# Attention scores in a single-core encoder block: both heads of a tile together, and K's low part against 64 rows of Q

## The chip, the core and the metric

The kernel runs on one core of one Trainium2 chip. The metric is the device time of one execution in microseconds. The arithmetic of the projections is done in fp32r matmuls on a high and a low part of each number, so that two or three passes give nearly float32 products.

## The reference

One layer of a hybrid encoder, 256 tokens, width 2048. The attention branch, which the change touches, has 16 heads of 64 on 4 key/value heads, a window of 128 tokens either way and a sink per head; around it stand large projections.

```python
u = rmsnorm(h, norm_mix_g)
z = u @ w_in                                   # 2048 -> 8704
b_a, c_a, v_a, q, k, v, gl_a, gl_b = split(z)
y_a = (b_a * centred_dwconv3(c_a * v_a, conv_a_w)) @ w_out_a
q, k = rope(q), rope(k)
scores = (q @ k.T) * HEAD_DIM ** -0.5          # masked to |kpos - qpos| <= 128
m = max(max(scores), sink)
p = exp(scores - m) / (sum(exp(scores - m)) + exp(sink - m))
y_b = (p @ v) @ w_o_attn
h = h + (sigmoid(gl_a + ba) * y_a + sigmoid(gl_b + bb) * y_b) @ w_mix_out
up = centred_dwconv3(rmsnorm(h) @ ffn_w_up, ffn_conv_w) + ffn_conv_b
h = h + (silu(a) * gv) @ ffn_w_down            # a, gv = halves of up
return rmsnorm(h, norm_final_g)
```

## The kernel before

**The projections.** Weights are streamed from HBM in chunks of eight 128x128 blocks. ScalarE rounds a chunk to fp32r (`whi`, L166), VectorE takes the rest (`wlo`, L177), and TensorE makes for each block one matmul of 512 columns with `whi` (L197: high and low part of the activations side by side) and one of 256 columns with `wlo` (L198). The last block of a job has its `whi` matmul in L202. `run` (from L105 on) walks over the chunks. After each chunk it raises `now` by one and calls `run_due`, which first advances the generators under way (each `yield` hands on to the next chunk) and then begins what is due at this chunk, in the order in which it was entered. Instructions go to each engine's queue in the order written.

**The attention.** A tile `t` (0 to 7) is a pair of heads `e` = 0, 1 that share their place in a 128-row block of Q. `rope` leaves for each head a tile in which rows `64*e` to `64*e+63` are the head's 64 dimensions and the other 64 rows are a copy of them. `rope_q` (L384 on) makes the first 64 rows the high part of Q and the other 64 the low part (L386, L390), so that one matmul over 128 rows of `qs` against `kh`, whose halves are both K's high part, gives (Q high + Q low) x K high. `kl`, K's low part, stands in both halves too. `att_scores(t, e)` multiplies, for each of two blocks `n` of 128 queries, `qs` with `kh` (L422) and then with `kl` (L423) into one bank of PSUM, `s0` or `s1` by head, with one buffer each. Then come the mask, the maximum, the exponential and the division (L428 to L444). `att_turn` transposes the probabilities (L452), `att_out` multiplies them with V (L465): there the two heads of a tile go to different halves of the output's partitions, so that each matmul uses 64 columns of the array.

**The order.** A table at the end of the attention's code enters the five steps of tile `t` at chunk 29 + 21t/4 (whole chunks, so 5 or 6 apart) plus 0 for `att_scores(t, 0)`, 3 for `att_scores(t, 1)`, 5 and 8 for the two turns, 10 for the output. They lie between the projections of `w_in`.

Of the kernel before, what the change touches and what calls it, by code (L numbers as in the profile page):

```python
# [7 lines left out]
F32 = mybir.dt.float32  # L8
# [6 lines left out]
P = 128  # L15
D = 2048
T = 256
# [34 lines left out]
def hybrid_block_kernel(ctx: ExitStack, tc: tile.TileContext, head, wide, xT, w_in, w_oa, w_o, w_mix, w_up, w_dn, vec, cst, out):  # L52
    nc = tc.nc
# [5 lines left out]
    aps = ctx.enter_context(tc.tile_pool(name="aps", bufs=1, space=PSUM))  # L59
# [9 lines left out]
    def col(i):  # L69
        return vt[:, i : i + 1]  # L70
# [17 lines left out]
    def at(n, fn):  # L88
        due.append((n, count[0], fn))
        count[0] += 1  # L90
# [257 lines left out]
    qs = p1.tile([P, 4, 2, 2, T], F32R, tag="qs", name="qs")  # L348
    kh = p1.tile([P, 2, 2, T], F32R, tag="kh", name="kh")
    kl = p1.tile([P, 2, 2, T], F32R, tag="kl", name="kl")  # L350
# [63 lines left out]
    probs = {}  # L414
    mask = ct[:, C_MASK : C_MASK + T]

    def att_scores(t, e):
        kv = t // 4
        sc = aps.tile([P, 2, T], F32, tag=f"s{e}", name=f"s{e}")
        for n in range(2):  # L420
            q = qs[:, t // 2, e, t % 2, n * P : (n + 1) * P]
            nc.tensor.matmul(sc[:, n, :], q, kh[:, e, kv, :], start=True, stop=False)  # L422
            nc.tensor.matmul(sc[:, n, :], q, kl[:, e, kv, :], start=False, stop=True)  # L423
        h = PAIRS[t][e]
        sink, ns = col(V_SINK + h), nsink[:, h : h + 1]
        flat = sc.rearrange("p n t -> p (n t)")

        nc.vector.tensor_tensor(flat[:, P : 3 * P], flat[:, P : 3 * P], mask, op=ALU.add)  # L428
        st = p1.tile([P, 8], F32, tag="st", name="st", bufs=4)
        mx, nm, den, es = (st[:, 2 * i : 2 * i + 2] for i in range(4))  # L430
        nc.vector.tensor_reduce(mx, sc, axis=AX.X, op=ALU.max, negate=True)
        nc.vector.tensor_scalar(nm, mx, HD**-0.5, ns, op0=ALU.mult, op1=ALU.min)
        yield 1
        p = p1.tile([P, 2, T], F32, tag="p", name="p", bufs=3)
        for n in range(2):
            nc.scalar.activation(
                p[:, n, :], sc[:, n, :], AF.Exp, bias=nm[:, n : n + 1], scale=HD**-0.5, accum_out=den[:, n : n + 1]
            )
        nc.scalar.activation(es, nm, AF.Exp, bias=sink)
        yield 1  # L440
        nc.vector.tensor_tensor(den, den, es, op=ALU.add)
        nc.vector.reciprocal(den, den)
        for n in range(2):
            nc.vector.tensor_scalar(p[:, n, :], p[:, n, :], den[:, n : n + 1], None, op0=ALU.mult)  # L444
        probs[t, e] = p

    def att_turn(t, e):
        p = probs.pop((t, e))
        tp = aps.tile([P, 2, T], F32, tag="tp", name="ptp")
        for b in range(2):  # L450
            for n in range(2):
                nc.tensor.transpose(tp[:, b, n * P : (n + 1) * P], p[:, n, b * P : (b + 1) * P], ident)  # L452
        yield 1
        pT = p1.tile([P, 2, T], F32, tag="pT", name="pT", bufs=2)
        nc.scalar.copy(pT, tp)
        probs[t, e] = pT

    def att_out(t):
        kv = t // 4
        o = aps.tile([P, 2 * T], F32, tag="av", name="av")  # L460
        pT = [probs.pop((t, e)) for e in range(2)]
        for b in range(2):
            for e in range(2):
                v0 = 128 * kv + 64 * e
                nc.tensor.matmul(  # L465
                    o[64 * e : 64 * e + 64, 0:T], vtok[:, b, v0 : v0 + HD], pT[e][:, b, :], start=b == 0, stop=b == 1
                )
        yield 1
        yield from split(box["B"][:, 8 + t, :], o[:, 0:T])
# [65 lines left out]
        at(40 + 4 * i, lambda i=i: nc.sync.dma_start(x[:, 4 * i : 4 * i + 4, :], xT[:, 4 * i : 4 * i + 4, :]))  # L535
    for t in range(8):
        for n, fn in (
            (0, lambda t=t: att_scores(t, 0)),
            (3, lambda t=t: att_scores(t, 1)),
            (5, lambda t=t: att_turn(t, 0)),  # L540
            (8, lambda t=t: att_turn(t, 1)),
            (10, lambda t=t: att_out(t)),
        ):
            at(29 + 21 * t // 4 + n, fn)
# [290 lines left out]
```

## Time and profile before

| | |
|---|---|
| median of 3 runs | 1354.29 us (1352.67 to 1354.65) |
| the profiled execution, its time | 1353.56 us |
| its span in the trace | 1351.8 us |
| mean granted TensorE clock | 0.998 of full |
| PE busy | 1340.5 us, 7687 instructions |
| PEld busy (weight loads, beside PE) | 1163.5 us |
| DVE busy | 971.5 us |
| ACT busy | 711.2 us |

The span is what the core's instructions take; 1.8 us lie around it. The scores are computed between 77 and 207 us of the span. A matmul's row in the trace begins when TensorE takes it up and its end is modelled, so that rows overlap: the time that a matmul costs is read from its start to the start of the next one, or from the chain, which cuts the rows where they overlap.

### The profile page before, as it was taken

To read this page: it belongs to the slowest core of one execution; us is meant where nothing else is said; L and a number is where in the kernel's file an instruction comes from. 1 tells how busy PE (TensorE), PEld (TensorE's weight loads), DVE (VectorE), ACT (ScalarE), POOL (GpSimd) and SP (SyncE) were. 2 spreads that over 40 slices of the span, in tenths; PEclk is the share of its full clock that TensorE was granted. 3 is DMA by queue.
4 is the path that set the end of the run, shared out by engine and by line. 5 is a ranking of instruction groups with operands and counts; after the bars stand their busy time and mean duration, and the time that the engine had idled before them with its cause. 6 is when DMAs were issued, how large, how long until landed. Compare 5 with 4: busy or idle time off the path is not lost.

```text
span 1351.8 us, 20512 instructions
## 1 busy us (share of the span) xinstructions
PE 1340.5 (99%) x7687; PEld 1163.5 (86%) x7687; DVE 971.5 (72%) x1544; ACT 711.2 (53%) x1120; POOL 58.6 (4%) x66
## 2 busy tenths in 40 slices
PE   9999999999999999999999999999999999999997
PEld 8888888888888888888888888888888888888886
DVE  7999887555557887668888888888888865555554
ACT  7656665544445554456555555555555544444441
POOL 0000000000000003420000000000000001001001
PEclk9999999999999999999999999999999999999999
DMA  8776545555555547547555555555555557656663
GB/s 296 231 226 197 188 154 178 184 186 186 187 186 187 187 133 239 186 135 235 186 187 186 187 184 188 186 187 185 186 185 187 169 155 234 187 180 187 187 188 100
DMA packets 75876, 254.23 MB, mean 188 GB/s; under 512 B 8704, under 2 KB 9088, under 8 KB 75776
## 3 DMA queue, kind: packets, MB, share of 16 engines
q1 hardware_dynamic: 75488, 252.52, 58.8%
q8 instruction: 60, 0.98, 0.3%
q10 hardware_dynamic: 288, 0.39, 0.1%
q14 instruction: 40, 0.33, 0.1%
HBM read 248.16 MB, written 2.10 MB: 185 GB/s over the span
## 4 chain that ended last, share of the span: by engine, by line
PE 99%; DVE 0%; DMA 0%; ACT 0%; issue 0%; POOLq 0%; DVEq 0%; ACTq 0%
PE ps L197 60%; PE ps L198 33%; PE ps L202 4%; PE av L465 1%; PE ptp L452 1%; PE ps L200 0%; PE s L423 0%; PE s L422 0%; DMA hd<-in_head_dram 0%; PE more L657 0%; POOLq L830 0%; DVE y L699 0%; DVE r L691 0%; DVE x L664 0%; PE nps L240 0%
## 5 line engine op out<-in xcount | busy, mean ns | idle before, releaser
L177 DVE TENSOR_TENSOR wlo<-raw,whi 128x1024 fp32r<-128x1024 f32 (+2 forms) x494 | 570.8, 1158 | 324.9 <-PE ps L198 230.5
L166 ACT CAST whi<-raw 128x1024 fp32r<-128x1024 f32 (+2 forms) x494 | 488.2, 989 | 349.2 <-PE ps L197 180.0
L197 PE MATMUL ps<-hs,whi 128*128 128x512 f32 x1320 | 470.1, 399 | 0.0
L198 PE MATMUL ps<-hs,wlo 128*128 128x256 f32 x1408 | 381.2, 281 | 0.0
L197 PE MATMUL ps<-xs,whi 128*128 128x512 f32 x1020 | 363.9, 399 | 0.6 <-DVE xs L320 0.6
L197 PEld LDWEIGHTS ps<-hs,whi 128*128 128x128 f32 x1320 | 248.1, 188 | 57.1
L198 PE MATMUL ps<-xs,wlo 128*128 128x256 f32 x1088 | 295.4, 281 | 0.0
L198 PEld LDWEIGHTS ps<-hs,wlo 128*128 128x128 f32 x1408 | 265.8, 189 | 8.9
L197 PEld LDWEIGHTS ps<-xs,whi 128*128 128x128 f32 x1020 | 192.3, 189 | 44.3 <-ACT whi L166 0.9
L198 PEld LDWEIGHTS ps<-xs,wlo 128*128 128x128 f32 x1088 | 206.1, 189 | 5.6 <-DVE wlo L177 0.3
L226 ACT COPY evb<-ps 128x256 f32<-128x256 f32 x188 | 69.7, 372 | 212.2 <-PE ps L202 208.5
L197 PE MATMUL ps<-actC,whi 128*128 128x512 f32 x405 | 143.8, 399 | 0.0
L198 PE MATMUL ps<-actC,wlo 128*128 128x256 f32 x448 | 122.3, 281 | 0.0
L197 PEld LDWEIGHTS ps<-actC,whi 128*128 128x128 f32 x405 | 76.1, 188 | 18.9
L197 PE MATMUL ps<-ms,whi 128*128 128x512 f32 x240 | 85.4, 399 | 0.0
L198 PEld LDWEIGHTS ps<-actC,wlo 128*128 128x128 f32 x448 | 84.7, 189 | 0.8
L197 PE MATMUL ps<-actA,whi 128*128 128x512 f32 x240 | 85.3, 398 | 0.0
L197 PE MATMUL ps<-ya_att,whi 128*128 128x512 f32 x224 | 80.4, 398 | 0.0
L230 DVE TENSOR_TENSOR evt<-ps,evb 128x256 f32<-128x256 f32 x178 | 74.5, 418 | 0.0
L198 PE MATMUL ps<-actA,wlo 128*128 128x256 f32 x256 | 71.1, 281 | 0.0
L198 PE MATMUL ps<-ms,wlo 128*128 128x256 f32 x256 | 69.3, 281 | 0.0
L198 PE MATMUL ps<-ya_att,wlo 128*128 128x256 f32 x256 | 66.6, 281 | 0.0
(149 smaller groups left out, 1159.1 us busy)
## 6 DMA issues: line engine op xcount, KB each, us to landing
raw<-in_w_up_dram SPq DMA_DIRECT2D x170, 512.0 KB, 4.5
raw<-in_w_in_dram SPq DMA_DIRECT2D x124, 512.0 KB, 4.7
raw<-in_w_dn_dram SPq DMA_DIRECT2D x70, 512.0 KB, 4.1
raw<-in_w_mix_dram SPq DMA_DIRECT2D x26, 512.0 KB, 4.8
raw<-in_w_dn_dram SPq DMA_DIRECT2D x36, 256.0 KB, 2.7
raw<-in_w_oa_dram SPq DMA_DIRECT2D x16, 512.0 KB, 3.6
raw<-in_w_o_dram SPq DMA_DIRECT2D x16, 512.0 KB, 3.6
raw<-in_wide_dram SPq DMA_DIRECT2D x15, 512.0 KB, 5.3
```

The lines of the kernel that those rows point to most:

```text
L166: nc.scalar.copy(his[c][:, a:b, :], raws[c](a, b))
L177: nc.vector.tensor_tensor(los[c][:, a:b, :], raw(a, b), his[c][:, a:b, :], op=ALU.subtract)
L197: nc.tensor.matmul(ps, hi[:, i, :], a, start=k == 0, stop=False)
L198: nc.tensor.matmul(ps[:, 0:T], lo[:, i, :], a[:, 0:T], start=False, stop=False)
L202: nc.tensor.matmul(ps, hi[:, i, :], a, start=False, stop=True)
L226: nc.scalar.copy(b, ps[:, T : 2 * T])
L230: nc.vector.tensor_tensor(dst, ps[:, 0:T], b, op=ALU.add)
L452: nc.tensor.transpose(tp[:, b, n * P : (n + 1) * P], p[:, n, b * P : (b + 1) * P], ident)
L465: nc.tensor.matmul(o[64 * e : 64 * e + 64, 0:T], vtok[:, b, v0 : v0 + HD], pT[e][:, b, :], start=b == 0, stop=b == 1)
```

## The change

Both heads' scores of a tile are issued in one step, `att_products(t)`, at the chunk at which head 0's were issued; the softmax of head 0 is begun at that chunk and that of head 1 three chunks later, as before. In `att_products` the four matmuls of a block `n` stand in the order K high for head 0, K high for head 1, K low for head 0, K low for head 1. The two with K low read 64 rows instead of 128, those with Q's high part (rows 0 to 63 for head 0, 64 to 127 for head 1), so that Q low x K low is no longer part of the scores. The program gives these two matmuls a tile of the array of 64 rows x 128 columns, one at row 0 and one at row 64.

```diff
-    def att_scores(t, e):
+    scores = {}
+
+    def att_products(t):
+
         kv = t // 4
-        sc = aps.tile([P, 2, T], F32, tag=f"s{e}", name=f"s{e}")
+        for e in range(2):
+            scores[t, e] = aps.tile([P, 2, T], F32, tag=f"s{e}", name=f"s{e}")
         for n in range(2):
-            q = qs[:, t // 2, e, t % 2, n * P : (n + 1) * P]
-            nc.tensor.matmul(sc[:, n, :], q, kh[:, e, kv, :], start=True, stop=False)
-            nc.tensor.matmul(sc[:, n, :], q, kl[:, e, kv, :], start=False, stop=True)
+            q = [qs[:, t // 2, e, t % 2, n * P : (n + 1) * P] for e in range(2)]
+            for e in range(2):
+                nc.tensor.matmul(scores[t, e][:, n, :], q[e], kh[:, e, kv, :], start=True, stop=False)
+            for e in range(2):
+                h = slice(64 * e, 64 * e + 64)
+                nc.tensor.matmul(scores[t, e][:, n, :], q[e][h], kl[h, e, kv, :], start=False, stop=True)
+
+    def att_softmax(t, e):
+        sc = scores.pop((t, e))
...
-            (0, lambda t=t: att_scores(t, 0)),
-            (3, lambda t=t: att_scores(t, 1)),
+            (0, lambda t=t: att_products(t)),
+            (0, lambda t=t: att_softmax(t, 0)),
+            (3, lambda t=t: att_softmax(t, 1)),
```

TensorE's queue at tile 0 before, where head 0's scores (`s_900`) stand between two projection matmuls:

```order
L198 MATMUL ps<-xs,wlo 128x256
L422 MATMUL s_900<-kh,qs 128x256
L423 MATMUL s_900<-kl,qs 128x256
L422 MATMUL s_900<-kh,qs 128x256
L423 MATMUL s_900<-kl,qs 128x256
L197 MATMUL ps<-xs,whi 128x512
```

The same place of TensorE's queue in the changed kernel, where L427 is the line with K high, L430 that with K low, and `s_901` head 1's scores:

```order
L198 MATMUL ps<-xs,wlo 128x256
L427 MATMUL s_900<-kh,qs 128x256
L427 MATMUL s_901<-kh,qs 128x256
L430 MATMUL s_900<-kl,qs 128x256
L430 MATMUL s_901<-kl,qs 128x256
L427 MATMUL s_900<-kh,qs 128x256
L427 MATMUL s_901<-kh,qs 128x256
L430 MATMUL s_900<-kl,qs 128x256
L430 MATMUL s_901<-kl,qs 128x256
L197 MATMUL ps<-xs,whi 128x512
```

The tile's eight matmuls now stand in one place, with the two of K low next to each other, twice in a tile. The piece of the difference on TensorE three chunks later, where head 1's scores (`s_1004`) stood:

```order
 L202 MATMUL ps<-xs,whi 128x512
-L422 MATMUL s_1004<-kh,qs 128x256
-L423 MATMUL s_1004<-kl,qs 128x256
-L422 MATMUL s_1004<-kh,qs 128x256
-L423 MATMUL s_1004<-kl,qs 128x256
 L197 MATMUL ps<-xs,whi 128x512
```

These four have moved to the place above, and nothing of the attention is left here. TensorE's queue of the changed kernel at tile 1, with the semaphores that it waits for (`Activation` is ScalarE's, `DVE` VectorE's; `s_1085` is the second use of the bank of head 1):

```order
L462 MATMUL ptp<-ct,p 128x128 x4
L427 MATMUL s_1084<-kh,qs 128x256
L427 MATMUL s_1085<-kh,qs 128x256 [waits DVE_49,Activation_49]
L430 MATMUL s_1084<-kl,qs 128x256
L430 MATMUL s_1085<-kl,qs 128x256
L427 MATMUL s_1084<-kh,qs 128x256
```

The first matmul of head 1 now waits here, five chunks after tile 0's, for the bank that tile 0's head 1 leaves free; before it stood three chunks later.

## Rows read from the trace of the kernel before

**Rows 1.** The page's first lines: busy time of each engine, and the chain of work that ended last, by engine and by line.
```profile
PE 1340.5 (99%) x7687; PEld 1163.5 (86%) x7687; DVE 971.5 (72%) x1544; ACT 711.2 (53%) x1120; POOL 58.6 (4%) x66
PE 99%; DVE 0%; DMA 0%; ACT 0%; issue 0%; POOLq 0%; DVEq 0%; ACTq 0%
PE ps L197 60%; PE ps L198 33%; PE ps L202 4%; PE av L465 1%; PE ptp L452 1%; PE ps L200 0%; PE s L423 0%; PE s L422 0%; DMA hd<-in_head_dram 0%; PE more L657 0%; POOLq L830 0%; DVE y L699 0%; DVE r L691 0%; DVE x L664 0%; PE nps L240 0%
```

**Rows 2.** The waits of TensorE's matmuls over the whole span, all of them: us in total, times, longest.
```profile
PE nps L679 <- ACT sq L678: 1.3, 1, 1.3
PE warm L287 <- DVE eps L282: 1.1, 1, 1.1
PE ps L197 <- DVE xs L320: 0.6, 1, 0.6
```

**Rows 3.** The matmuls of the scores, lines L422 and L423 over the whole span: durations in ns (least, median, most), first and last start, form.
```profile
L422 PE MATMUL s<-kh,qs x32: 278/282/365, 77.3 to 206.7; 128*128 128x256 f32 x32
L423 PE MATMUL s<-kl,qs x32: 279/280/286, 77.4 to 206.8; 128*128 128x256 f32 x32
```

**Rows 4.** The chain at tile 0's head 0: start, share of the chain in us, what.
```profile
77.10 0.23 PE ps L197
77.33 0.12 PE ps L198
77.45 0.12 PE s L422
77.56 0.12 PE s L423
77.69 0.12 PE s L422
77.80 0.12 PE s L423
77.92 0.23 PE ps L197
```

**Rows 5.** The timeline of weight loads at the same place: start, us, instruction.
```profile
77.29 0.19 PEld L423 LDWEIGHTS s<-kl,qs 128*128 128x128 f32 x1
77.40 0.19 PEld L422 LDWEIGHTS s<-kh,qs 128*128 128x128 f32 x1
```

**Rows 6.** Matmuls of the output product of a tile (L465, 64 columns of the array): three rows of the timeline with two matmuls each; the eight of that product in the chain; the line's durations in ns over the whole span.
```profile
159.31 0.39 PE L465 MATMUL av<-pT,vtok 128*64 128x256 f32 x2
159.52 0.39 PE L465 MATMUL av<-pT,vtok 128*64 128x256 f32 x2
159.74 0.39 PE L465 MATMUL av<-pT,vtok 128*64 128x256 f32 x2
...
159.11 1.01 PE av L465 x8
...
L465 PE MATMUL av<-pT,vtok x64: 379/379/431, 108.3 to 229.3; 128*64 128x256 f32 x64
```

**Rows 7.** Timeline of TensorE where that output product follows a projection matmul: matmuls, then weight loads. In brackets is the idle time before an instruction.
```profile
158.72 0.39 PE L202 MATMUL ps<-xs,whi 128*128 128x512 f32 x1
159.04 0.44 PE L465 MATMUL av<-pT,vtok 128*64 128x256 f32 x2
...
158.60 0.19 PEld L202 LDWEIGHTS ps<-xs,whi 128*128 128x128 f32 x1
159.04 0.20 PEld L465 LDWEIGHTS av<-pT,vtok 128*64 128x64 f32 x4 [0.25 <-issue]
```

**Rows 8.** Another output product, which follows a matmul of 256 columns.
```profile
108.05 0.28 PE L198 MATMUL ps<-xs,wlo 128*128 128x256 f32 x1
108.25 0.44 PE L465 MATMUL av<-pT,vtok 128*64 128x256 f32 x2
```

**Rows 9.** Timeline of TensorE where that output product ends and a projection matmul follows: matmuls, then weight loads.
```profile
160.06 0.50 PE L197 MATMUL ps<-xs,whi 128*128 128x512 f32 x1
160.39 0.28 PE L198 MATMUL ps<-xs,wlo 128*128 128x256 f32 x1
160.51 0.40 PE L197 MATMUL ps<-xs,whi 128*128 128x512 f32 x1
...
160.05 0.19 PEld L197 LDWEIGHTS ps<-xs,whi 128*128 128x128 f32 x1 [0.39 <-issue]
160.16 0.19 PEld L198 LDWEIGHTS ps<-xs,wlo 128*128 128x128 f32 x1
```

**Rows 10.** Waits of the weight loads over the whole span, those with no releaser in the profile: us in total, times, longest.
```profile
PEld ptp L452 <- issue: 2.3, 6, 0.4
PEld av L465 <- issue: 2.0, 8, 0.3
PEld ps L197 <- issue: 0.8, 2, 0.4
```

**Rows 11.** Where the bank of head 1 comes free: the second exponential of tile 0's and tile 1's head 1 on ScalarE, each followed by the first score matmul of the next tile on TensorE; last, the end of the making of tile 0's Q for head 1 on VectorE.
```profile
90.44 0.46 ACT L436 ACTIVATE p<-s,st 128x256 f32<-128x256 f32 x1
92.57 0.36 PE L422 MATMUL s<-kh,qs 128*128 128x256 f32 x1
107.64 0.47 ACT L436 ACTIVATE p<-s,st 128x256 f32<-128x256 f32 x1
109.69 0.36 PE L422 MATMUL s<-kh,qs 128*128 128x256 f32 x1
73.86 0.68 DVE L390 TENSOR_TENSOR qs<-two,qs 64x512 fp32r<-64x512 f32 x1
```

## The prediction

> **What bounds the kernel now.** I read the page's busy times first, then the chain of work that ended last, then the waits of TensorE, and last the timeline around the scores. TensorE's matmuls fill 99% of the span, and the chain is made of them almost alone [rows 1]. TensorE waited for another engine three times in the whole span, at its beginning and its end [rows 2]; between 70 and 240 us, where the attention lies, it never did. So nothing that VectorE, ScalarE or a queue does there sets the end, unless the change makes TensorE wait for it. What TensorE spends more or less on the scores goes to the end one for one.
>
> What a score matmul costs is not the 280 ns of its row [rows 3], since rows overlap, but its step in the chain: 0.118 us, four of them in 0.47 us (77.45 to 77.92), and 0.23 us for a projection matmul of 512 columns [rows 4]. The weights of the next matmul are loaded while the one before streams: the loads start at 77.29 and 77.40, in the middle of matmuls that use all 128 rows too [rows 5]. So in this stretch the loads cost nothing of their own. All 64 score matmuls together are 64 x 0.118 = 7.6 us; half of them, those with K low, are 3.8 us. That is all that the change can touch.
>
> **The change, part by part.**
>
> *Fewer rows.* A matmul with K low reads 64 rows of Q instead of 128 and still streams the same 256 columns of K. The price of a matmul here follows the columns: 0.118 for 256, 0.23 for 512 [rows 4], so I cost the shorter contraction at nothing. The trace has no matmul on 64 rows. Were the price to follow the rows after all, it would be halved, and a pair one after the other would cost 0.118, what the overlap of the next part gives as well; both together would give another 16 x 0.06 = 1 us, which I leave out, since no row has columns at less.
>
> *Two heads at once.* The two K-low matmuls of a block sit on different rows and write different banks. Whether two such matmuls overlap is shown for columns: in the output product two matmuls on two halves of the columns stand in one row of 0.39 us, and the next pair begins 0.21 us later [rows 6]; the row of one of them alone is 0.38. So a pair there costs what one costs, and the eight took 1.01 us in the chain. I take the same for the rows: a pair costs 0.125 (0.118 and the few ns by which two on different columns are apart) instead of 2 x 0.118 = 0.236. There are 2 blocks x 8 tiles = 16 pairs, so this saves 16 x 0.11 = 1.8 us. The other bound is that they don't overlap: 0.
>
> *Going into the smaller tile and out again.* This is the term that decides. The array is used as 128 x 128 all around, and the order puts each pair of K low between matmuls on the whole array, so it goes over to 64-row tiles and back 16 times. The rows before show such a passage for the output product, and it isn't free. On the way in, the matmul at 158.72 (512 columns, 0.23) should be followed at 158.95, but the next starts at 159.04, and its weights are loaded only then, after 0.25 us in which the load idled for nothing that the profile shows [rows 7]. After a matmul of 256 columns it is the same: 108.05 + 0.118 = 108.17, and the next one starts at 108.25 [rows 8]. That is 0.09 us in which the array empties. Then the load itself is no longer hidden: the first pair's row is 0.44 against 0.39 later, and the second pair starts 0.27 instead of 0.21 after it [rows 6, 7], 0.05 us for weights of 64 columns. On the way out, the last pair starts at 159.74, would be done with its columns at 159.95, and the next matmul starts at 160.06: 0.10 us. Its weights, 128 columns now, are loaded at that point as well (0.39 idle before the load), its row is 0.50 instead of 0.40, and the one behind it starts 0.33 instead of 0.23 later: 0.10 us for the load [rows 9]. It is no accident of one tile: the weight loads idle this way on all 8 ways in and all 8 ways out (6 into transposes, 2 into projections), and elsewhere on none [rows 10].
>
> For a pair of K low the weights have 128 columns, so its load in the open is that of the way out, 0.10, and I take the two loads of a pair as one beside the other, as in the output product, where four loads are begun within 0.20 us [rows 7]. One pair then costs 0.09 (empty) + 0.10 (load) + 0.125 (stream) + 0.10 (empty) + 0.10 (load of the next K-high weights) = 0.515 us where 0.236 stood: +0.28. Sixteen times is +4.5 us. The second K-high matmul behind it has its load hidden again.
>
> The bounds of this term: below, no passage costs anything (the rows know only the passage to columns, and rows might differ), −1.8 us in all; between, the array empties but both loads hide in that time, 0.19 + 0.125 − 0.236 = +0.08, +1.3 us; above, the pair's two matmuls or their two loads come one after the other, 0.10 to 0.11 more each, +6.2 us with one of the two and +7.9 with both. I take +4.5, by the nearest rows, the same engine 2 us to 30 us away from the scores.
>
> The Trainium skill has rules on either side. "TensorEngine Tiling (Array Packing)", section Key Properties, states that a change of the tiling mode drains TensorE, and counts row tiles and column tiles as modes alike; the idle 0.25 and 0.39 us agree for columns, and no row here shows it for 64-row tiles. By that rule alone the sum stays at +4.5. "TensorE: Matmul & The Clock Gate", Part 3, gives instead a packed span of one matmul and some 4 ns for each further tile, with no price for the passage; by that the sum would be about −1.8 us, the first rival below. The same part has weight loads overlap a running matmul only where the row groups differ, which this trace contradicts: loads and matmuls on all 128 rows overlap at 77.29.
>
> *Head 1 earlier.* Its four matmuls move forward by three chunks. TensorE does them at another time; nothing is added. What is queued behind them is the projection, which waits for nothing else. VectorE's and ScalarE's instructions keep their order, and head 1's softmax finds its scores ready earlier, which costs and gives nothing, since neither sets the end. No DMA moves.
>
> *The new wait.* Head 1's bank has one buffer, so its matmuls at tile t+1 now wait for the exponential of tile t's head 1 which was begun about two chunks before, and the projection stands in the queue behind them. The second exponential of tile 0 begins at 90.44 and ends at 90.90, and tile 1's scores start at 92.57; at the next tile it is 107.64 + 0.47 = 108.11 against 109.69 [rows 11]. The cover is 1.6 us in the tightest case, and later tiles have more. Since TensorE gets later and ScalarE doesn't, it grows. Q for head 1 of tile 0 is ready at 73.86 + 0.68 = 74.54, 2.7 us before 77.28. I cost both at nothing. Were the cover gone, TensorE would stand still for each microsecond by which the exponential is late, up to seven times.
>
> **The sum.** −1.8 + 16 x (0.09 + 0.10 + 0.10 + 0.10) = −1.8 + 6.3 = +4.5 us. On the profiled execution (span 1351.8, time 1353.56) that is 1356.3 and 1358.1. The median of the runs shown, 1354.29, is 0.73 us above that execution, so the forecast for a median is 1354.29 + 4.5 = 1358.8 us, +0.33%. I count as no change what lies within 0.2%, 2.7 us.
>
> **The rivals.**
>
> *The passage to row tiles is free* (not slower). For it: half of the rows of the array are left alone by each of the two loads, and PSUM's side doesn't change, other than with columns. Against it: the output product, the only change of tile in the trace, idles every time. It gives −1.8 us, 1352.5, within 0.2%. The point from which it decides: up to 0.11 us for a way in and out the change is no loss; at 0.28 us it is 0.2% slower; the output product's rows make it 0.39.
>
> *The array empties, but the loads hide.* For it: 0.09 and 0.10 us are about as long as a load of 128 columns takes (0.11 between two loads at 160.05 and 160.16 [rows 9]). Against it: in the passages that the trace has, the load begins only when the matmul does [rows 7, 9]. +1.3 us, 1355.6.
>
> *The pair doesn't overlap, or its loads don't.* For it: two loads of 128 columns need twice the weights of the output product's pair. Against it: that pair's loads start together. +6.2 us, 1360.5, up to 1362.2.
>
> *TensorE waits for the exponential.* It needs ScalarE to be over 1.6 us later than now at tile 1 or 2. Nothing in the change delays it; a whole chunk late, twice, would be +2.5 us on top.
>
> **How the numbers follow.** Forecast (+3.5 to +5.5) 0.63; pair or loads one after the other 0.11; wait for the exponential on top 0.02; loads hidden 0.09; free passage 0.13; anything faster by over 0.2% 0.02, since the change can save no more than 1.8 us. Slower is 0.76, the same 0.22, faster 0.02. The range from 1355.2 to 1360.9 takes in the hidden loads at +1.3 and one of the two things in series at +6.2, and leaves out the free passage.
>
> **What would show it.** In the changed trace: weight loads of L430 and of the L427 or L197 behind them with 0.2 to 0.4 us idle before them, about 32 times; two L430 matmuls starting together; the step from the second L427 to the first L430 about 0.2 us instead of 0.118, and the first matmul after a pair with a row longer by 0.1. TensorE's waits for other engines should stay as in [rows 2]. Loads of L430 begun while L427 streams would make the forecast wrong.

## The result and the profile after

The changed kernel took 1358.89 us in the median of 6 runs (1357.5 to 1359.69), the kernel before 1354.47 in the median of 6: 4.42 us more. The ratio of the means is 1.0035 (95% interval 1.0024 to 1.0045, that is 3.3 to 6.1 us). The forecast was 1358.8. The profiled execution took 1358.38 us, its span is 1356.6, 4.8 more than before.

The page's busy times and the chain by engine, which answer to [rows 1]:

```profile
PE 1344.4 (99%) x7687; PEld 1162.4 (86%) x7687; DVE 971.8 (72%) x1544; ACT 710.9 (52%) x1120; POOL 57.6 (4%) x66
PE 98%; DMA 0%; DVE 0%; ACT 0%; POOLq 0%; issue 0%; SPq 0%; DVEq 0%; ACTq 0%
```

TensorE is still the chain, with the same count of matmuls. All its waits for other engines, which answer to [rows 2] (us in total, times, longest):

```profile
PE ps L197 <- ACT whi L166: 1.3, 1, 1.3
PE warm L287 <- DVE eps L282: 1.1, 1, 1.1
PE nps L690 <- ACT sq L689: 1.0, 1, 1.0
PE ps L197 <- DVE xs L320: 0.4, 1, 0.4
```

One wait is new, once, for a chunk of weights at 8.3 us; it lies far ahead of the scores and has no part in the difference, since in the chain the first score matmul stands at 77.38 here (below) and at 77.45 before [rows 4]. No score matmul waits for another engine.

The timeline at tile 0, matmuls and then weight loads (start, us, instruction; x2 are two neighbours of one line in one row). L427 is K high, L430 K low:

```profile
77.10 0.28 PE L198 MATMUL ps<-xs,wlo 128*128 128x256 f32 x1
77.21 0.40 PE L427 MATMUL s<-kh,qs 128*128 128x256 f32 x2
77.54 0.38 PE L430 MATMUL s<-kl,qs 64*128 64x256 f32 x2
77.85 0.50 PE L427 MATMUL s<-kh,qs 128*128 128x256 f32 x2
78.29 0.38 PE L430 MATMUL s<-kl,qs 64*128 64x256 f32 x2
78.60 0.50 PE L197 MATMUL ps<-xs,whi 128*128 128x512 f32 x1
78.94 0.28 PE L198 MATMUL ps<-xs,wlo 128*128 128x256 f32 x1
...
77.10 0.31 PEld L427 LDWEIGHTS s<-kh,qs 128*128 128x128 f32 x2
77.54 0.19 PEld L430 LDWEIGHTS s<-kl,qs 64*128 64x128 f32 x2
77.85 0.30 PEld L427 LDWEIGHTS s<-kh,qs 128*128 128x128 f32 x2
78.28 0.19 PEld L430 LDWEIGHTS s<-kl,qs 64*128 64x128 f32 x2
```

The two L427 from 77.21 on stream until 77.45 (2 x 0.118), and L430 starts at 77.54. Its loads begin at the same moment, both of them, and are not hidden: the pair's row is 0.38 where such a matmul has 0.28 otherwise. Both matmuls of the pair fit into that 0.38, so they run side by side. L427 follows 0.31 later, again with its load at its own start, and its row of two is 0.50 instead of 0.40; the same at 78.60, where L197 has 0.50 and L198 comes 0.34 behind it instead of 0.23.

The chain of the same stretch (start, share in us), which answers to [rows 4]:

```profile
77.38 0.23 PE s L427 x2
77.61 0.31 PE s L430 x2
77.92 0.43 PE s L427 x2
78.36 0.31 PE s L430 x2
78.67 0.43 PE ps L197
79.10 0.12 PE ps L198
```

From 77.38 to 79.10 the eight score matmuls and the L197 behind them take 1.72 us. Before, they were 8 x 0.118 + 0.23 = 1.17. That is 0.55 us a tile and 4.4 us for eight tiles, the whole difference. The other tiles agree: by the starts of the matmuls in the traces, each of the eight takes 0.53 to 0.55 us more here than in the run of the order alone below, which has the same order, 4.3 us together. This sum, from the first score matmul of a tile to the end of the L197 behind its last, is the measure for the experiments below.

### The profile page after: what moved, and what is told of

Read it like the earlier page. It is cut to its first block, busy times and chain, and to the rows that moved or that the text cites. A ratio compares the mean times of both kernels' runs of the same rounds, so it can differ in the third digit from the quotient of the medians.

```text
span 1356.6 us, 20510 instructions
## 1 busy us (share of the span) xinstructions
PE 1344.4 (99%) x7687; PEld 1162.4 (86%) x7687; DVE 971.8 (72%) x1544; ACT 710.9 (52%) x1120; POOL 57.6 (4%) x66
## 4 chain that ended last, share of the span: by engine, by line
PE 98%; DMA 0%; DVE 0%; ACT 0%; POOLq 0%; issue 0%; SPq 0%; DVEq 0%; ACTq 0%
PE ps L197 60%; PE ps L198 32%; PE ps L202 4%; PE av L475 1%; PE ptp L462 1%; DMA raw<-in_wide_dram 0%; PE s L427 0%; PE ps L200 0%; PE s L430 0%; PE more L668 0%; POOLq L841 0%; DVE y L710 0%; DVE r L702 0%; DVE x L675 0%; ACT whi L166 0%
## 5 line engine op out<-in xcount | busy, mean ns | idle before, releaser
L197 PE MATMUL ps<-hs,whi 128*128 128x512 f32 x1320 | 470.1, 399 | 0.0
L198 PE MATMUL ps<-hs,wlo 128*128 128x256 f32 x1408 | 381.2, 281 | 0.0
L197 PE MATMUL ps<-xs,whi 128*128 128x512 f32 x1020 | 364.4, 399 | 1.8 <-ACT whi L166 1.3
L197 PEld LDWEIGHTS ps<-hs,whi 128*128 128x128 f32 x1320 | 248.1, 188 | 57.1
L198 PE MATMUL ps<-xs,wlo 128*128 128x256 f32 x1088 | 295.3, 281 | 0.0
L198 PEld LDWEIGHTS ps<-hs,wlo 128*128 128x128 f32 x1408 | 265.8, 189 | 8.9
L197 PEld LDWEIGHTS ps<-xs,whi 128*128 128x128 f32 x1020 | 191.5, 188 | 46.7 <-ACT whi L166 2.3
L198 PEld LDWEIGHTS ps<-xs,wlo 128*128 128x128 f32 x1088 | 205.4, 189 | 6.1 <-DVE wlo L177 0.6
L197 PE MATMUL ps<-actC,whi 128*128 128x512 f32 x405 | 143.8, 399 | 0.0
L198 PE MATMUL ps<-actC,wlo 128*128 128x256 f32 x448 | 122.3, 281 | 0.0
L197 PEld LDWEIGHTS ps<-actC,whi 128*128 128x128 f32 x405 | 76.1, 188 | 18.9
L197 PE MATMUL ps<-ms,whi 128*128 128x512 f32 x240 | 85.4, 399 | 0.0
L198 PEld LDWEIGHTS ps<-actC,wlo 128*128 128x128 f32 x448 | 84.7, 189 | 0.8
L197 PE MATMUL ps<-actA,whi 128*128 128x512 f32 x240 | 85.3, 398 | 0.0
L197 PE MATMUL ps<-ya_att,whi 128*128 128x512 f32 x224 | 80.4, 398 | 0.0
L198 PE MATMUL ps<-actA,wlo 128*128 128x256 f32 x256 | 71.1, 281 | 0.0
L198 PE MATMUL ps<-ms,wlo 128*128 128x256 f32 x256 | 69.3, 281 | 0.0
L198 PE MATMUL ps<-ya_att,wlo 128*128 128x256 f32 x256 | 66.7, 281 | 0.0
```

Source lines behind the costliest of these rows:

```text
L197: nc.tensor.matmul(ps, hi[:, i, :], a, start=k == 0, stop=False)
L198: nc.tensor.matmul(ps[:, 0:T], lo[:, i, :], a[:, 0:T], start=False, stop=False)
```

## The experiments

A passage is the way of the array to 64-row tiles and back; the time in between, on these tiles, is called a visit. Theory: each passage costs 0.39 us, as the array empties twice and loads weights in the open twice, and a pair side by side saves 0.11. Rival A: the new order or its wait costs the time. Rival B: each matmul on 64 rows is dearer in itself. Rival C: the price is that of two tiles at work at once. All runs were timed in five rounds beside the kernel before, which had 1354.33 us in the median for the first four and 1354.18 for the last two.

### The order alone

```diff
             for e in range(2):
-                h = slice(64 * e, 64 * e + 64)
-                nc.tensor.matmul(scores[t, e][:, n, :], q[e][h], kl[h, e, kv, :], start=False, stop=True)
+                nc.tensor.matmul(scores[t, e][:, n, :], q[e], kl[:, e, kv, :], start=False, stop=True)
```

> The changed kernel's order, both heads of a tile together, but K low against all 128 rows of Q as before, so the whole array is used throughout. Theory (the 16 passages to 64-row tiles and back cost 0.39 us each and the overlap of a pair saves 0.11 each): no passage, no overlap, so the time of the kernel before, 1354.3, within 1 us. Rival A (the cost comes from the new order: head 1's bank asked for three chunks earlier, or the projection queued behind eight matmuls instead of four): +4.5 us, 1358.8.

Measured: 1354.49 us, ratio 1.0000 (0.9991 to 1.0009). The chain at tile 0, where L429 is K low:

```profile
78.12 0.24 PE s L427 x2
78.36 0.24 PE s L429 x2
78.60 0.24 PE s L427 x2
78.83 0.23 PE s L429 x2
79.07 0.23 PE ps L197
79.31 0.12 PE ps L198
```

1.19 us, against 1.17 before, and the interval of the time is 1.2 us either way. Rival A, which asked for 4.5, falls: the order, the earlier use of head 1's bank and eight matmuls in one place cost nothing that shows.

### The 64 rows alone, in the order of before

```diff
-            nc.tensor.matmul(sc[:, n, :], q, kl[:, e, kv, :], start=False, stop=True)
+            h = slice(64 * e, 64 * e + 64)
+            nc.tensor.matmul(sc[:, n, :], q[h], kl[h, e, kv, :], start=False, stop=True)
```

> The order of the kernel before, each head by itself, but K low against the 64 rows of Q's high part: 32 single matmuls on a 64-row tile, each between two matmuls on the whole array. Theory: 32 passages at 0.39 us and nothing saved by overlap, +12.5 us, 1366.8. Rival B (the price is of each 64-row matmul and not of the passage: 32 matmuls in the changed kernel as here, 0.28 / 2 each on top of what they were): the same +4.5 us as the changed kernel, 1358.8. Rival C (the price arises only where two tiles of the array run at once): 0, 1354.3.

Measured: 1367.9 us, 13.6 more than before, ratio 1.0100 (1.0086 to 1.0114). The chain at tile 0's head 0, where L424 is K low:

```profile
78.99 0.11 PE s L422
79.11 0.31 PE s L424
79.42 0.32 PE s L422
79.73 0.31 PE s L424
80.04 0.43 PE ps L197
80.48 0.12 PE ps L198
```

1.49 us from 78.99 to 80.48, against 4 x 0.118 + 0.23 = 0.70 before: 0.79 for two passages, 0.39 each, and 16 x 0.79 = 12.6 us for all (12.4 when the steps of all 16 heads in the trace are summed). The interval (11.6 to 15.4 us) holds it. A single matmul on 64 rows has the same 0.31 in the chain as a pair in the changed kernel. Rival C, which asked for no loss here, falls, and so does B, which asked for 4.5.

### Half as many passages

```diff
-        for n in range(2):
-            q = [qs[:, t // 2, e, t % 2, n * P : (n + 1) * P] for e in range(2)]
-            for e in range(2):
-                nc.tensor.matmul(scores[t, e][:, n, :], q[e], kh[:, e, kv, :], start=True, stop=False)
-            for e in range(2):
-                h = slice(64 * e, 64 * e + 64)
-                nc.tensor.matmul(scores[t, e][:, n, :], q[e][h], kl[h, e, kv, :], start=False, stop=True)
+        q = lambda e, n: qs[:, t // 2, e, t % 2, n * P : (n + 1) * P]
+        for n in range(2):
+            for e in range(2):
+                nc.tensor.matmul(scores[t, e][:, n, :], q(e, n), kh[:, e, kv, :], start=n == 0, stop=False)
+        for n in range(2):
+            for e in range(2):
+                h = slice(64 * e, 64 * e + 64)
+                nc.tensor.matmul(scores[t, e][:, n, :], q(e, n)[h], kl[h, e, kv, :], start=False, stop=n == 1)
```

> As the changed kernel, but in each tile first the four matmuls with K high, then the four with K low: the same 32 matmuls on 64 rows and the same 16 pairs, but 8 passages instead of 16. Theory: 8 x 0.39 - 16 x 0.11 = +1.3 us, 1355.6, that is 3.1 us less than the changed kernel; the second pair's loads should begin while the first pair streams. Rival B (a price of each 64-row matmul): +4.5 us, 1358.8.

Measured: 1355.07 us, 0.7 more than before, ratio 1.0006 (0.9997 to 1.0015). The chain at tile 0, where L431 is K low:

```profile
77.58 0.47 PE s L427 x4
78.06 0.43 PE s L431 x4
78.49 0.43 PE ps L197
78.92 0.12 PE ps L198
```

1.34 us, 0.17 more than the 1.17 before, which makes 1.3 for eight tiles; the interval (−0.4 to 2.0 us) holds that and zero. The second pair adds 0.12 to the first one's 0.31, so inside a visit nothing is paid again: the four loads of a visit stand in one row of 0.30 us from 77.98 on, so that those of the second pair begin while the first pair streams. The same 32 matmuls on 64 rows cost 3.7 us less in the time and 3.1 us less in the chain with half of the passages, which rival B can't give. Nor can a price of each pair or single on 64 rows, which the run with the single matmuls alone would still allow: the 16 pairs are the same here.

### The same passages without overlap

```diff
             for e in range(2):
-                h = slice(64 * e, 64 * e + 64)
+                h = slice(0, 64)
```

> As the changed kernel, but head 1's K low too is multiplied with rows 0 to 63 of its Q, which are Q's low part there, so that Q high x K low is left out for the eight heads 1 and Q low x K low stands in its place. Both matmuls of a pair then sit on the same rows of the array. The 16 passages stay. Theory: the pair costs 2 x 0.118 instead of 0.125, so 16 x 0.11 = 1.8 us more than the changed kernel: +6.3 us, 1360.6. Rival (a pair's two starts 3 ns apart in the trace are only modelled, and the two run one after the other anyway): no difference from the changed kernel, +4.5 us, 1358.8.

Measured: 1361.25 us, 6.9 more than before, ratio 1.0049 (1.0036 to 1.0062). The chain at tile 0:

```profile
78.50 0.23 PE s L427 x2
78.73 0.43 PE s L430 x2
79.16 0.43 PE s L427 x2
79.59 0.43 PE s L430 x2
80.02 0.43 PE ps L197
80.45 0.12 PE ps L198
```

The weight loads of the first pair in the timeline:

```profile
78.66 0.29 PEld L430 LDWEIGHTS s<-kl,qs 64*128 64x128 f32 x2
```

The pair has 0.43 where it had 0.31 on different rows: 0.12 more, one matmul's stream. The stretch is 1.95 us, so 0.78 a tile more than before, 6.2 us in all. The interval of the time (4.9 to 8.4 us) overlaps with that of the changed kernel (3.3 to 6.1), so the times alone leave some doubt; the chain decides. So in the changed kernel the pair did overlap, and 16 x 0.12 = 1.9 us of gain are in its 4.4. The two loads now begin one after the other (their row is 0.29 us, where it was 0.19 on different rows). That the second load didn't add 0.10 to the step as well shows that on 64 rows a load hides behind a matmul on the same rows, as on the whole array.

### Fewer rows without another tile

```diff
             for e in range(2):
-                h = slice(64 * e, 64 * e + 64)
+                h = slice(0, 96)
```

> As the changed kernel, but the two K-low matmuls of a pair read rows 0 to 95 of Q instead of 64 rows, a count that the program puts on the whole array, so the tile doesn't change. (For head 0 this adds half of Q low x K low, for head 1 it takes Q low and half of Q high instead of Q high.) Theory (the price is that of changing the tile, not of contracting over fewer rows than 128): as the kernel before, 1354.3, within 1 us, with the weight loads of K low begun while K high streams. Rival (fewer rows than 128 are what empties the array): +4.5 us without the overlap, that is about +6.3, 1360.6.

Measured: 1354.51 us, ratio 1.0002 (0.9993 to 1.0011). The durations of K low's matmuls over the whole span (ns least, median, most; first and last start; form), and the weight loads at tile 0:

```profile
L430 PE MATMUL s<-kl,qs x32: 279/283/288, 77.9 to 199.0; 96*128 96x256 f32 x32
...
77.58 0.31 PEld L427 LDWEIGHTS s<-kh,qs 128*128 128x128 f32 x2
77.82 0.31 PEld L430 LDWEIGHTS s<-kl,qs 96*128 96x128 f32 x2
```

The median of 283 ns is that of K high on 128 rows in the same run, 282, and the loads of K low run on behind those of K high, each beside a matmul. The rival falls: contracting over 96 rows costs nothing and gives nothing. The price comes with the 64-row tile.

### A whole tile of the attention on 64 rows

```diff
-            for e in range(2):
-                nc.tensor.matmul(scores[t, e][:, n, :], q[e], kh[:, e, kv, :], start=True, stop=False)
-            for e in range(2):
-                h = slice(64 * e, 64 * e + 64)
-                nc.tensor.matmul(scores[t, e][:, n, :], q[e][h], kl[h, e, kv, :], start=False, stop=True)
+            for k in (kh, kl):
+                for e in range(2):
+                    h = slice(64 * e, 64 * e + 64)
+                    nc.tensor.matmul(scores[t, e][:, n, :], q[e][h], k[h, e, kv, :], start=k is kh, stop=k is kl)
```

> As the changed kernel, but K high too is multiplied with the 64 rows of Q's high part alone, so that Q low x K high is left out, and all eight matmuls of a tile of the attention are four pairs on 64-row tiles: 8 passages instead of 16, 32 pairs instead of 16. Theory: 8 x 0.39 - 32 x 0.11 = -0.4 us, 1353.9, not to be told from no change: even with every pair overlapped, the passage eats the gain. Rival (a price of each 64-row matmul, 0.14 for each): 64 x 0.14 = +9 us, 1363. Within a visit a pair should follow the one before after 0.12 us in place of the 0.22 after a passage.

Measured: 1354.23 us, ratio 1.0000 (0.9992 to 1.0009). The timeline at tile 0, K high and K low both in L429:

```profile
78.20 0.39 PE L429 MATMUL s<-kh,qs 64*128 64x256 f32 x2
78.42 0.28 PE L429 MATMUL s<-kl,qs 64*128 64x256 f32 x2
78.54 0.28 PE L429 MATMUL s<-kh,qs 64*128 64x256 f32 x2
78.66 0.28 PE L429 MATMUL s<-kl,qs 64*128 64x256 f32 x2
78.87 0.50 PE L197 MATMUL ps<-xs,whi 128*128 128x512 f32 x1
```

After the first pair, 0.22 on, the pairs follow each other by 0.12, two matmuls at a time. The rival, which asked for 1363, falls. The chain:

```profile
78.27 0.67 PE s L429 x8
78.94 0.43 PE ps L197
```

Emptying, load, four pairs and the way out come to 1.10 us with the L197, against 1.17 before: though every pair overlaps, the visit gains 0.07 us, 0.6 for eight tiles. The interval of the time (−1.1 to 1.2 us) doesn't tell that from nothing. None of the versions beats the kernel before by anything that its time shows.

## Why the prediction was right

**TensorE bounds, and what it spends goes to the end.** Right: 0.55 us a tile in the chain and 4.42 us in the time.

**Fewer rows at nothing.** Right: 96 rows on the whole array changed neither a row nor the time. On 64 rows, 256 columns cost what they cost on 128: a further pair in a visit took 0.12 us, and a single matmul had the same 0.31 in the chain as a pair. Were a matmul on 64 rows cheaper and the two of a pair one after the other, the single one would have had less.

**The overlap, −1.8 us.** Right: without it the changed kernel lost 6.9 instead of 4.4 us; 0.12 a pair in the chain makes 1.9 us.

**The passage, 0.39 us.** This term was taken from the other kind of tile, columns, and it held for rows, which no row of the trace before had shown. By pieces, from the timeline after: empty 0.09 on the way in (77.45 to 77.54), load 0.10 (0.38 against 0.28), load 0.10 on the way out (0.50 against 0.40). The 0.31 from L430 to L427 is load 0.10 and stream 0.12, which leaves 0.09 for the way out where I had 0.10. So a pair cost 0.50 instead of 0.515, and 16 x (0.50 − 0.236) = 4.2 us; the chain has 4.4, and the difference is the rounding of the pieces. The single matmuls measured the passage by itself: 0.39.

By the Trainium skill, "TensorEngine Tiling (Array Packing)", section Key Properties, a change of tiling mode drains TensorE; the trace after agrees for row tiles, 0.09 us in and out, and adds 0.10 us of load each way. The packed span of "TensorE: Matmul & The Clock Gate", Part 3, agrees with the pair itself, whose row of 0.38 us is that of a single one, and leaves out the passage, which here is over three times what the pair gains.

**Head 1 earlier, and its bank.** Right in the sum, wrong in one reason. I said that the cover of the exponential grows, since ScalarE doesn't get later. The second exponential of tile 0's head 1 and the first matmuls of tile 1, as in [rows 11]:

```profile
91.28 0.46 ACT L446 ACTIVATE p<-s,st 128x256 f32<-128x256 f32 x1
93.09 0.48 PE L427 MATMUL s<-kh,qs 128*128 128x256 f32 x2
```

It ends at 91.74, 0.84 later than before, while TensorE came 0.52 later: the cover shrank from 1.67 to 1.35 us. At the next tile it did grow, from 1.58 to 1.74 (108.94 to 110.69). It was enough at every tile, and the order alone, with the same wait, cost nothing. Why ScalarE came later at the first of them was not followed up.

**The signs in the trace.** The step from the second L427 to the first L430 (0.21), the longer rows and the pairs were as said. Wrong was the idle time of 0.2 to 0.4 us before each load. The loads before L430 end at 77.41 and those of L430 begin at 77.54, 0.13, and on the way out it is 0.12 (77.73 to 77.85). I had carried that figure over from visits with a matmul of 512 columns in front [rows 7] or with longer streams inside [rows 9]; behind two short matmuls the last load ends later, and less is seen of the same emptying. In the last run, where a projection matmul of 512 columns stands two places ahead of the visit, the idle time before the first load is 0.25 us again. An idle time before a load is no measure of the passage; the step between matmuls is.

**What stays open.** For the single matmuls and for the pair without overlap the time was 1.0 and 0.7 us above what the chain at tile 0 gives for all tiles. Summed over all tiles of the traces, the stretches give 12.4 and 6.2 us, so the rest isn't in the scores, and it lies within the intervals. Some of it stands ahead of them in the two profiled executions, where the first score matmul starts at 78.83 and 78.34, against 77.28 before. The runs show that the array empties and that loads aren't begun early at a passage; what in the engine holds them back they don't show.

## What to carry to other kernels

Small matmuls side by side on tiles of the array can pay only where enough of them stand together: here a passage cost 0.39 us and a pair of 256 columns gave back 0.12, so that a visit breaks even between three and four pairs. One pair a visit lost 4.4 us, two lost 0.7, and four came out even; no run had more. The order of the matmuls decides, not their number: group them before choosing smaller tiles, or leave them on the whole array, where a contraction over 96 rows cost the same as a full one. A price can be read from the kernel before if any instruction there makes the same kind of passage; here it was the output product of the attention, for columns, and it held for rows.

## What the runs showed of the hardware that was not expected

The emptying after a pair of short fp32r matmuls was 0.09 us, the same on both ways, where the output product had shown 0.10 on the way out. And a matmul with 96 rows ran beside the loads of its neighbours on the whole array like one with 128, 283 against 282 ns a row in that run, while 64 rows brought the passage with them.
